# Last normalisation of each branch on ScalarE, o^T split beside the last heads, one more step ahead of the compressed transposes

## Chip, core and metric

The kernel runs on one core of a Trainium2 chip. The metric is the device time of one execution in microseconds (us). The engines are TensorE (PE in the profile; its weight loads are PEld), VectorE (DVE), ScalarE (ACT), GpSimd (POOL) and SyncE (SP, which issues most DMAs). Each engine takes its instructions in the order in which the program has put them into its queue.

## What is computed

A decoder trunk of two layers on x (512 tokens, width 1024). Each layer is a token mixer of two parallel branches, RetNet retention and NSA sparse attention, and then a SwiGLU FFN. The change touches the NSA branch alone. Cut to that branch, the reference is:

```python
lc = einsum('bghqd,bgnd->bghqn', qx, kc) * scale + head_bias(dc)      # compressed keys, 31 per group
pc = masked_softmax(lc, dc >= 0);  oc = einsum('bghqn,bgnd->bghqd', pc, vc)
ps = masked_softmax(ls, ds >= 0);  os_ = einsum('bghqm,bgqmd->bghqd', ps, vsel)   # selected blocks
pw = masked_softmax(lw, in_window); ow = einsum('bghql,bgld->bghqd', pw, vw)      # sliding window
out = gx[..., 0:1] * oc + gx[..., 1:2] * os_ + gx[..., 2:3] * ow
y_nsa = o_n @ w_o_nsa[i]
```

With 512 tokens, 8 blocks of 64 and a top-8 choice, every block is selected, and the window of 512 covers every earlier token. So the selected and the window branch are causal softmaxes over all tokens, each with its own keys and values.

## The kernel before

Every float32 product is made of three matmuls of a high and a low half (`mm3`, lines 122 to 124: weight high by activation high, low by high, high by low). The halves come from `split` (lines 79 and 80): ScalarE rounds a copy to the high half, VectorE subtracts to get the low half. `cut` does that to the weights that a DMA brought, into tiles `wh` and `wl`, of which three pairs exist.

`nsa` runs 16 heads in a software pipeline, one iteration a head. In an iteration stand the scores of head n (`nsa_scores`), the transposes and value products of head n-1 (`nsa_values`), the end of head n-2 (`nsa_finish`), and, to keep TensorE busy, pieces of other projections (`gate_steps`, the tiles f). `merge` interleaves these generators: a generator that is said to have so many steps gets its steps at even distances in its span of the iteration. The framework's scheduler then fixes each engine's queue.

- `nsa_scores`: for each of two branches and four blocks of 128 query rows, the scores go to a PSUM bank a (two exist), VectorE adds the bias and finds the maximum (line 509), ScalarE makes the exponential and its sum (line 510). The four blocks are 128, 256, 384 and 512 keys wide. After the last, VectorE turns the sums into factors sm (lines 533 to 536) and multiplies all eight blocks by them (line 540).
- `nsa_values`: TensorE transposes the normalised p into a bank t (line 560), ScalarE and VectorE split it into two tiles pt, and TensorE multiplies them with the values into a bank o (lines 552 and 553, high and low half).
- `nsa_cmp`, once for four heads (a quad): the compressed branch. Its scores are transposed, biased on VectorE (line 458), the maximum is found (line 462, VectorE) and subtracted (line 463, GpSimd), the exponential made (line 465, ScalarE), masked (line 466, GpSimd), summed (line 469, VectorE), and multiplied by the gate over the sum (line 476, GpSimd). Then TensorE transposes the result cz (line 480), and it is split into pc. The plan gives it 10 steps.
- `nsa_finish`: one more product with pc into bank o (line 574), then the two halves of the bank are added into the tile ot (lines 578 and 579). Two heads share one ot, so eight of them hold o^T.

After the loop, the eight ot are split into oh and ol (called from `nsa`, executed at lines 79 and 80), and the projection with w_o_nsa begins, eight times 24 matmuls.

Of the kernel before, what the change touches and what calls it, by code (L numbers as in the profile page):

```python
# [22 lines left out]
HN = 16  # L23
# [8 lines left out]
class Builder:  # L32
# [403 lines left out]
    def nsa_cmp(self, quad, qs, heads, pc):  # L436
        nc = self.nc
        ps = self.mm()
        for s, (qh, ql) in enumerate(qs):
            kz = self.kcz[s % 2][:, 96 - 32 * s : 224 - 32 * s]  # L440
            nc.tensor.matmul(ps, kz, qh, start=s == 0, stop=False)
            nc.tensor.matmul(ps, kz, ql, start=False, stop=s == 3)
        yield
        st = self.u("cst")
        nc.scalar.activation(st, ps, AF.Copy)
        pt = self.tp()
        for i in range(NT):
            nc.tensor.transpose(pt[:, i * P : (i + 1) * P], st[:, i * P : (i + 1) * P], self.ident)
        yield
        z = self.u("cz")  # L450
        z4 = z.rearrange("p (i s n) -> p i s n", i=NT, s=4)
        p4 = pt.rearrange("p (i s n) -> p i s n", i=NT, s=4)
        nc.gpsimd.memset(z, NEG)
        for i in range(NT):
            n = min(NCMP, 7 + 8 * i)
            for s in range(4):
                bias = self.backwards(heads[4 * quad + s]["strip"], 96 + P * i, n, 16)
                nc.vector.tensor_tensor(z4[:, i, s, :n], p4[:, i, s, :n], bias, ALU.add)
            yield
        z3 = z.rearrange("p (c n) -> p c n", n=32)  # L460
        mx = self.small("cmx", 16)
        nc.vector.tensor_reduce(mx, z3, AX.X, ALU.max)
        nc.gpsimd.tensor_tensor(z3, z3, mx[:, :, None].broadcast_to([P, 16, 32]), ALU.subtract)
        yield
        nc.scalar.activation(z, z, AF.Exp)
        nc.gpsimd.tensor_tensor(z4, z4, self.cmask[:, :, None, :].broadcast_to([P, NT, 4, 32]), ALU.mult)
        yield
        sm = self.small("csm", 16)
        nc.vector.tensor_reduce(sm, z3, AX.X, ALU.add)
        nc.vector.tensor_scalar(sm, sm, 1e-30, None, ALU.max)  # L470
        nc.vector.reciprocal(sm, sm)
        s4 = sm.rearrange("p (i a b) -> p i a b", a=2, b=2)
        for b in range(2):
            h0 = 2 * quad + 8 * b
            nc.vector.tensor_tensor(s4[:, :, :, b], s4[:, :, :, b], self.gate[:, :, h0 : h0 + 2, 0], ALU.mult)
        nc.gpsimd.tensor_tensor(z3, z3, sm[:, :, None].broadcast_to([P, 16, 32]), ALU.mult)
        yield
        pt2 = self.tp()
        for i in range(NT):
            nc.tensor.transpose(pt2[:, i * P : (i + 1) * P], z[:, i * P : (i + 1) * P], self.ident)  # L480
        yield

        for r, o in ((slice(0, 64), slice(64, P)), (slice(64, P), slice(0, 64))):
            x = self.u("pc", F32R)
            self.split(x[r], x[o], pt2[r])
            pc.append(x)


    def nsa_scores(self, st):
        nc = self.nc  # L490
        g = st["h"] // 8
        qh, ql = st["q"]
        ks = self.ks[g]
        strip = st["strip"]
        pr = st["p"] = [[None] * NT for _ in range(2)]
        nmx = self.small("nmx", 2 * NT)
        sm = self.small("sm", 2 * NT)


        p1 = self.tile("p", NPB)  # L500
        for br in range(2):
            p2, p3 = self.tile("p", NPB), self.tile("p", NPB)
            pr[br] = [p2[:, 3 * P :], p1[:, br * 2 * P : (br + 1) * 2 * P], p2[:, : 3 * P], p3]

        def soft(br, i, src):
            w = (i + 1) * P
            p = pr[br][i]
            c = slice(br * NT + i, br * NT + i + 1)
            nc.vector.tensor_tensor_reduce(p, src, self.backwards(strip, w - 1, w), -1.0, BIG, ALU.add, ALU.min, nmx[:, c])  # L509
            nc.scalar.activation(p, p, AF.Exp, scale=-1.0, bias=nmx[:, c], accum_out=sm[:, c])  # L510

        for i in range(2):
            w = (i + 1) * P
            ts = slice(i * P, w)
            ps = self.bank("a")
            dst = ps[:, : 2 * w].rearrange("p (b n) -> p b n", b=2)
            nc.tensor.matmul(dst, qh[:, ts], ks[:, :, :w], start=True, stop=False)
            nc.tensor.matmul(dst, ql[:, ts], ks[:, :, :w], start=False, stop=True)
            for br in range(2):
                soft(br, i, ps[:, br * w : (br + 1) * w])  # L520
            yield

        for br in range(2):
            for i in range(2, NT):
                w = (i + 1) * P
                ts = slice(i * P, w)
                ps = self.bank("a")
                nc.tensor.matmul(ps[:, :w], qh[:, ts], ks[:, br, :w], start=True, stop=False)  # L528
                nc.tensor.matmul(ps[:, :w], ql[:, ts], ks[:, br, :w], start=False, stop=True)  # L529
                soft(br, i, ps[:, :w])  # L530
                yield

        nc.vector.tensor_scalar(sm, sm, 1e-30, None, ALU.max)
        nc.vector.reciprocal(sm, sm)
        sv = sm.rearrange("p (b t) -> p b t", b=2)
        nc.vector.tensor_tensor(sv, sv, self.gate[:, :, st["h"], 1:].rearrange("p t b -> p b t"), ALU.mult)
        for br in range(2):
            for i in range(NT):
                c = br * NT + i
                nc.vector.tensor_scalar(pr[br][i], pr[br][i], sm[:, c : c + 1], None, ALU.mult)  # L540


    def nsa_values(self, st):
# [27 lines left out]
    def nsa_finish(self, st):  # L571
        nc = self.nc
        po, b, s = st["po"], st["h"] // 8, st["s"]
        nc.tensor.matmul(po, self.vc[:, b, s % 2], st["pc"][s // 2], start=False, stop=True)
        if b == 0:
            self.ot = self.u("ot")
        dst = self.ot[64 * b : 64 * b + 64]
        nc.scalar.activation(dst, po[64:128], AF.Copy)
        nc.vector.tensor_tensor(dst, po[0:64], dst, ALU.add)
        yield  # L580
        if b == 1:
            self.os.append(self.ot)

    def gate_steps(self, l, h):

# [42 lines left out]
    def nsa(self, l, h):  # L628
# [2 lines left out]
        q0 = self.nsa_q(l, h, 0, qs[0])  # L631
        self.ks, self.vs, self.gate = self.nsa_kv(l, h, q0)
        self.cycle = NCYCLE
        self.os = []
        heads = []
        fill = self.gate_steps(l, h)

        pcs = [[] for _ in range(4)]

        prep, plan = {}, [(1, 1, lambda: self.nsa_cmp(0, qs[0], heads, pcs[0]), 10)]  # L640
        for quad in range(1, 4):
            n = 4 * quad
            plan.append((n - QAT[0], QAT[1], lambda quad=quad: self.nsa_q(l, h, quad, qs[quad]), 18))
            plan.append((n, 1, lambda quad=quad: self.nsa_cmp(quad, qs[quad], heads, pcs[quad]), 10))
        for n0, span, make, steps in plan:
            g = make()
            for i in range(span):
# [5 lines left out]
        for n in range(HN + 2):  # L653
            gens = []
            if n == 0 or n % 4 == 3 and n + 1 < HN:
                for m in range(4):
                    st = heads[(n + 3) // 4 * 4 + m]
                    st["strip"] = self.bias_strip(st["h"])
            if n < HN:
                heads[n]["q"] = qs[n // 4][n % 4]  # L660
                gens.append((self.nsa_scores(heads[n]), 6, *AT["scores"]))
            if 0 < n <= HN:
                gens.append((self.nsa_values(heads[n - 1]), 8 + LAG, *AT["values"]))
            if n > 1:
                gens.append((self.nsa_finish(heads[n - 2]), 1, *AT["finish"]))
            gens.append((self.take(fill, FILL[n]), FILL[n], *AT["fill"]))
            gens += prep.get(n, [])
            self.merge(gens)
        for _ in fill:
            pass  # L670
        self.cycle = CYCLE
        w = self.a["w_o_nsa"][l]
        os = []
        for ot in self.os:
            os.append((self.u("oh", F32R), self.u("ol", F32R)))
            self.split(*os[-1], ot)
        for c in range(4):
            wv = self.chunk([(lambda v, g=g: v[g * 64 : g * 64 + 64], w[g * 512 : g * 512 + 512, c * 256 : c * 256 + 256]
                              .rearrange("(t d) n -> d t n", d=64)) for g in range(2)], KD, 256)
            for j in range(2):  # L680
                ps = self.proj_t(wv, j, os)
                yt = self.u("yn")
                nc.vector.scalar_tensor_tensor(yt, self.ld("gb", self.gs[KD + 2 * c + j]), 1.0, ps, ALU.add, ALU.mult)
                nc.scalar.dma_start(self.ys[2 * c + j], yt)
# [353 lines left out]
```

## Time and profile before

| | us |
|---|---|
| median of 3 runs (2425.92 to 2429.57) | 2428.91 |
| the profiled execution, its own time | 2427.7 |
| span of the profiled execution, first to last instruction | 2425.8 |
| TensorE busy in the span | 2371.8 (98%) |
| VectorE busy | 1410.7 (58%) |
| ScalarE busy | 1029.9 (42%) |
| GpSimd busy | 258.8 (11%) |

The profile gives each engine's busy time. Matmuls overlap in TensorE's pipeline, and their ends are modelled, so that two matmuls that start 0.23 us apart are each shown as 0.39 us. The distance of starts is the pace. The chain of work that ended last lies to 89% on TensorE, to 6% on VectorE and to 3% on ScalarE. The heads of the first layer run from about 85 to 416 us, those of the second from about 1285 to 1613 us; the projections of o^T follow right behind.

### The profile page before, as it was taken

The page shows a single profiled execution, that of the slowest core. Times are in us where ns is not written, and L with a number is a line of the kernel's source. Part 1 is how long each engine was busy: PE and PEld are TensorE (multiplying, and loading weights), DVE is VectorE, ACT ScalarE, POOL GpSimd, SP SyncE. Part 2 cuts the span into 40 slices and gives each one's busy share as a digit, 9 for nine tenths or more (in the row PEclk, how much of TensorE's full clock was granted, in tenths as well). Part 3 has the DMA queues.
Part 4 walks back from the last instruction along what each step waited for, and adds up shares of the span by engine and source line. Part 5 has one row for each costly group of instructions (what it writes and reads, how often), then busy time and mean ns, then how long its engine had stood idle before and what let it go on. Part 6 is the DMA issues. An engine that isn't in the chain of part 4 may idle for free.

```text
span 2425.8 us, 29172 instructions
## 1 busy us (share of the span) xinstructions
PE 2371.8 (98%) x11042; PEld 1938.4 (80%) x11042; DVE 1410.7 (58%) x2779; ACT 1029.9 (42%) x1862; POOL 258.8 (11%) x224
## 2 busy tenths in 40 slices
PE   7999999999999999999989999999999999999998
PEld 5877777888887888888878777778888878888887
DVE  6788887354574643333577888853555755434334
ACT  5676675233333422222356766742333333322222
POOL 2000000010020110110200000001100202101010
PEclk9999999999999999999999999999999999999999
DMA  7533124522342522322544322244233534223221
GB/s 209 149 89 84 57 74 100 166 90 91 109 148 88 166 89 91 101 94 94 147 142 125 96 68 65 79 110 146 92 102 98 164 114 135 87 87 104 87 96 61
DMA packets 234173, 260.37 MB, mean 107 GB/s; under 512 B 42213, under 2 KB 178437, under 8 KB 234032
## 3 DMA queue, kind: packets, MB, share of 16 engines
q1 hardware_dynamic: 220688, 236.93, 32.3%
q10 hardware_dynamic: 13152, 21.37, 2.4%
q8 instruction: 87, 1.43, 0.2%
q14 instruction: 54, 0.44, 0.1%
q0 software_dynamic: 192, 0.21, 0.0%
HBM read 235.36 MB, written 23.11 MB: 107 GB/s over the span
## 4 chain that ended last, share of the span: by engine, by line
PE 89%; DVE 6%; ACT 3%; issue 1%; POOL 1%; DMA 0%; SPq 0%; POOLq 0%; ACTq 0%; DVEq 0%
PE f L122 11%; PE f L123 11%; PE f L124 11%; PE o L123 8%; PE a L123 8%; PE o L122 8%; PE a L122 8%; PE o L124 8%; PE a L124 7%; PE t L560 2%; DVE p L540 1%; PE o L553 1%; PE o L552 1%; DVE wl L80 1%; PE a L528 1%
## 5 line engine op out<-in xcount | busy, mean ns | idle before, releaser
L79 ACT ACTIVATE wh<-wr 128x1024 fp32r<-128x1024 f32 (+3 forms) x406 | 397.9, 981 | 972.4 <-PE f L123 255.3
L80 DVE TENSOR_TENSOR wl<-wr,wh 128x1024 fp32r<-128x1024 f32 (+3 forms) x406 | 464.0, 1147 | 225.1 <-ACT wh L79 222.1
L122 PE MATMUL f<-hh,wh 128*128 128x512 f32 x936 | 373.9, 399 | 3.0 <-ACT wh L79 2.9
L123 PE MATMUL f<-hl,wh 128*128 128x512 f32 x936 | 371.0, 396 | 0.0
L124 PE MATMUL f<-hh,wl 128*128 128x512 f32 x936 | 369.3, 395 | 1.2 <-DVE wl L80 1.1
L124 PEld LDWEIGHTS f<-hh,wl 128*128 128x128 f32 x936 | 176.9, 189 | 41.5 <-DVE wl L80 3.6
L122 PEld LDWEIGHTS f<-hh,wh 128*128 128x128 f32 x936 | 177.0, 189 | 38.2 <-ACT wh L79 4.7
L123 PEld LDWEIGHTS f<-hl,wh 128*128 128x128 f32 x936 | 177.3, 189 | 30.5
L510 ACT ACTIVATE p<-p,nmx 128x512 f32<-128x512 f32 (+3 forms) x256 | 142.4, 557 | 67.1 <-DVE nmx L509 64.9
L80 DVE TENSOR_TENSOR pt<-t,pt 128x512 fp32r<-128x512 f32 (+3 forms) x256 | 123.2, 485 | 51.0 <-ACT pt L79 49.5
L79 ACT ACTIVATE pt<-t 128x512 fp32r<-128x512 f32 (+3 forms) x256 | 109.1, 429 | 76.0 <-PE t L560 73.0
L862 POOL TENSOR_TENSOR fa<-fa,rb 128x512 f32<-128x512 f32 x44 | 77.5, 1762 | 562.3 <-ACT fa L861 562.3
L123 PE MATMUL a<-hl,wh 128*128 128x512 f32 x336 | 132.5, 394 | 0.0
L122 PE MATMUL a<-hh,wh 128*128 128x512 f32 x336 | 132.2, 394 | 0.0
L509 DVE CUSTOM_DVE_ANT_0 p<-a,strip 128x512 f32<-128x512 f32 (+3 forms) x256 | 120.2, 484 | 19.4 <-PE a L529 12.0
L124 PE MATMUL a<-hh,wl 128*128 128x512 f32 x336 | 131.2, 390 | 0.0
L123 PE MATMUL o<-hl,wh 128*128 128x512 f32 x328 | 129.3, 394 | 0.0
L122 PE MATMUL o<-hh,wh 128*128 128x512 f32 x328 | 128.9, 393 | 0.0
L124 PE MATMUL o<-hh,wl 128*128 128x512 f32 x328 | 128.0, 390 | 0.0
L560 PE MATMUL t<-ident,p 128*128 128x128 f32 x640 | 113.5, 273 | 0.2
L560 PEld LDWEIGHTS t<-ident,p 128*128 128x128 f32 x640 | 80.5, 140 | 25.3 <-issue 3.1
L552 PE MATMUL o<-pt,vs 128*128 128x512 f32 (+3 forms) x256 | 91.5, 361 | 1.5 <-ACT pt L79 1.5
(404 smaller groups left out, 4832.4 us busy)
## 6 DMA issues: line engine op xcount, KB each, us to landing
wr<-in_w_in SPq DMA_DIRECT2D x66, 1024.0 KB, 5.3
wr<-in_w_ffn_in SPq DMA_DIRECT2D x44, 1024.0 KB, 5.1
wr<-in_w_ffn_out SPq DMA_DIRECT2D x18, 1024.0 KB, 5.0
wr<-in_w_o_ret SPq DMA_DIRECT2D x16, 1024.0 KB, 5.1
wr<-in_w_in SPq DMA_DIRECT2D x36, 256.0 KB, 4.6
strip<-bv SPq DMA_DIRECT2D x32, 256.0 KB, 4.4
gs<-mt ACTq DMA_DIRECT2D x32, 256.0 KB, 2.0
wr<-in_w_o_nsa SPq DMA_DIRECT2D x16, 512.0 KB, 6.5
```

Of the source, the lines that this page charges most:

```text
L79: self.nc.scalar.activation(hi, src, AF.Copy)
L80: (eng or self.nc.vector).tensor_sub(lo, src, hi.bitcast(F32))
L122: self.nc.tensor.matmul(ps, lh, rh, start=start and i == 0, stop=False)
L123: self.nc.tensor.matmul(ps, lh, rl, start=False, stop=False)
L124: self.nc.tensor.matmul(ps, ll, rh, start=False, stop=stop and i == n - 1)
L509: nc.vector.tensor_tensor_reduce(p, src, self.backwards(strip, w - 1, w), -1.0, BIG, ALU.add, ALU.min, nmx[:, c])
L510: nc.scalar.activation(p, p, AF.Exp, scale=-1.0, bias=nmx[:, c], accum_out=sm[:, c])
L528: nc.tensor.matmul(ps[:, :w], qh[:, ts], ks[:, br, :w], start=True, stop=False)
L540: nc.vector.tensor_scalar(pr[br][i], pr[br][i], sm[:, c : c + 1], None, ALU.mult)
L552: nc.tensor.matmul(po[:, j * P :], lhs, th, start=br == 0 and j == 0, stop=False)
L560: nc.tensor.transpose(pt[:, (i - j) * P : (i - j + 1) * P], pr[br][i][:, j * P : (j + 1) * P], self.ident)
L862: nc.gpsimd.tensor_mul(t, t, self.rb)
```

## The change

1. In `nsa_scores` the widest block of each branch (512 keys, two a head) is multiplied by its factor on ScalarE (an activation Copy with a column as scale) and not on VectorE.
2. A new generator `nsa_os` splits parts of o^T. It runs as one more generator in the last two iterations (up to part 3 in the first of them, up to part 6 in the second); the other two parts are split behind the loop.
3. `nsa_cmp` yields twice ahead of its transposes, and the plan gives it 11 steps.

```diff
         nc.gpsimd.tensor_tensor(z3, z3, sm[:, :, None].broadcast_to([P, 16, 32]), ALU.mult)
         yield
+        yield
         pt2 = self.tp()
...
-                nc.vector.tensor_scalar(pr[br][i], pr[br][i], sm[:, c : c + 1], None, ALU.mult)
+                if i == NT - 1:
+                    nc.scalar.activation(pr[br][i], pr[br][i], AF.Copy, scale=sm[:, c : c + 1])
+                else:
+                    nc.vector.tensor_scalar(pr[br][i], pr[br][i], sm[:, c : c + 1], None, ALU.mult)
...
+    def nsa_os(self, upto):
+
+        for n in range(len(self.oss), upto):
+            self.oss.append((self.u("oh", F32R), self.u("ol", F32R)))
+            self.split(*self.oss[n], self.os[n])
+            yield
...
-        prep, plan = {}, [(1, 1, lambda: self.nsa_cmp(0, qs[0], heads, pcs[0]), 10)]
+        prep, plan = {}, [(1, 1, lambda: self.nsa_cmp(0, qs[0], heads, pcs[0]), 11)]
...
-            plan.append((n, 1, lambda quad=quad: self.nsa_cmp(quad, qs[quad], heads, pcs[quad]), 10))
+            plan.append((n, 1, lambda quad=quad: self.nsa_cmp(quad, qs[quad], heads, pcs[quad]), 11))
...
+            if n >= HN:
+                upto = 3 * (n - HN + 1)
+                gens.append((self.nsa_os(upto), upto, 0, 1))
             self.merge(gens)
...
-        os = []
-        for ot in self.os:
-            os.append((self.u("oh", F32R), self.u("ol", F32R)))
-            self.split(*os[-1], ot)
+        for _ in self.nsa_os(HN // 2):
+            pass
...
-                ps = self.proj_t(wv, j, os)
+                ps = self.proj_t(wv, j, self.oss)
```

The scheduler moves instructions with it. TensorE where the projection of o^T begins in the first layer (oh and ol are the halves of o^T; o, a and f behind L122 to L124 are the banks that are written), before:

```order
L124 MATMUL f_4390<-hh_153,wl_4340 128x512
L122 MATMUL o_4467<-oh_4424,wh_4459 128x512
L122 MATMUL a_4497<-oh_4424,wh_4463 128x512
L122 MATMUL f_4538<-oh_4424,wh_4530 128x512
L123 MATMUL o_4467<-ol_4425,wh_4459 128x512
L124 MATMUL o_4467<-oh_4424,wl_4460 128x512
L122 MATMUL o_4467<-oh_4428,wh_4459 128x512
```

and now:

```order
L124 MATMUL f_4410<-hh_153,wl_4348 128x512
L122 MATMUL o_4467<-oh_4249,wh_4459 128x512
L123 MATMUL o_4467<-ol_4250,wh_4459 128x512
L124 MATMUL o_4467<-oh_4249,wl_4460 128x512
L122 MATMUL o_4467<-oh_4319,wh_4459 128x512
L123 MATMUL o_4467<-ol_4320,wh_4459 128x512
L124 MATMUL o_4467<-oh_4319,wl_4460 128x512
```

The first output is now made in one go, where three outputs were begun side by side before.

VectorE at the second quad of the first layer, from the normalisation to the sum of the compressed branch, before:

```order
L536 TENSOR_TENSOR sm_1653<-sm_1653,gate_624 128x8
L80 TENSOR_TENSOR wl_2070<-wr_2067,wh_2069 128x1024
L540 TENSOR_SCALAR p_1655<-p_1655,sm_1653 128x128
L540 TENSOR_SCALAR p_1654<-p_1654,sm_1653 128x256
L540 TENSOR_SCALAR p_1655<-p_1655,sm_1653 128x384
L540 TENSOR_SCALAR p_1656<-p_1656,sm_1653 128x512
L540 TENSOR_SCALAR p_1657<-p_1657,sm_1653 128x128
L540 TENSOR_SCALAR p_1654<-p_1654,sm_1653 128x256
L540 TENSOR_SCALAR p_1657<-p_1657,sm_1653 128x384
L540 TENSOR_SCALAR p_1658<-p_1658,sm_1653 128x512
L80 TENSOR_TENSOR pt_1852<-t_1849,pt_1851 128x128
L579 TENSOR_TENSOR ot_1858<-o_1426,ot_1858 64x512
```

and now:

```order
L80 TENSOR_TENSOR wl_2070<-wr_2067,wh_2069 128x1024
L80 TENSOR_TENSOR pt_1812<-t_1808,pt_1811 128x256
L534 TENSOR_SCALAR sm_1653<-sm_1653 128x8
L535 RECIPROCAL sm_1653<-sm_1653 128x8
L537 TENSOR_TENSOR sm_1653<-sm_1653,gate_624 128x8
L544 TENSOR_SCALAR p_1655<-p_1655,sm_1653 128x128
L544 TENSOR_SCALAR p_1654<-p_1654,sm_1653 128x256
L544 TENSOR_SCALAR p_1655<-p_1655,sm_1653 128x384
L544 TENSOR_SCALAR p_1657<-p_1657,sm_1653 128x128
L544 TENSOR_SCALAR p_1654<-p_1654,sm_1653 128x256
L544 TENSOR_SCALAR p_1657<-p_1657,sm_1653 128x384
L469 TENSOR_REDUCE csm_1876<-cz_1725 128x16
```

The two blocks of 512 have left the run, and the sum csm follows it at once; before it stood behind the split of pt and the sum ot.

TensorE at the same quad, up to the transposes of the compressed result cz, before:

```order
L122 MATMUL f_1838<-hh_153,wh_1830 128x512
L123 MATMUL f_1838<-hl_154,wh_1830 128x512
L528 MATMUL a_1951<-ks_251,qh_1412 128x384
L529 MATMUL a_1951<-ks_251,ql_1413 128x384
L124 MATMUL f_1838<-hh_153,wl_1831 128x512
L122 MATMUL f_1976<-hh_117,wh_1834 128x512
L123 MATMUL f_1976<-hl_118,wh_1834 128x512
L480 MATMUL t_1883<-ident,cz_1728 128x128 x4
```

and now:

```order
L124 MATMUL f_1842<-hh_149,wl_1835 128x512
L529 MATMUL a_1951<-ks_251,qh_1412 128x384
L530 MATMUL a_1951<-ks_251,ql_1413 128x384
L122 MATMUL f_1842<-hh_153,wh_1834 128x512
L481 MATMUL t_1883<-ident,cz_1725 128x128 x4
```

Four matmuls of 512 columns that stood ahead of the transposes stand behind them now. At the fourth quad the same happens; at the first and the third the transposes keep their place.

## Rows read from the trace of the kernel before

**Rows 1.** Three stretches: bounds, length, then busy time (instructions) of each engine
```profile
85.00:420.00 335.00, 325.36 (x1666) 263.43 (x1664) 271.26 (x770) 219.03 (x521) 15.71 (x15) 1.00 0.32 88
420.00:520.00 100.00, 100.00 (x436) 81.63 (x437) 46.59 (x67) 28.17 (x37) 9.33 (x9) 0.99 0.44 137
...
1285.00:1617.00 332.00, 322.36 (x1654) 261.29 (x1652) 268.35 (x761) 217.51 (x516) 15.70 (x15) 1.00 0.32 88
```

**Rows 2.** TensorE's waits, 85 to 420 us: for whom, total us, times, longest
```profile
PE o L553 <- DVE pt L80: 3.0, 3, 1.7
PE a L528 <- DVE nmx L509: 2.1, 2, 1.4
PE o L122 <- ACT oh L79: 2.0, 1, 2.0
...
PE t L480 <- POOL cz L476: 0.7, 3, 0.2
PE o L123 <- DVE ol L80: 0.4, 1, 0.4
```

**Rows 3.** TensorE's timeline around the projection's begin, both layers (start, us, instruction, [idle])
```profile
416.09 0.40 PE L124 MATMUL f<-hh,wl 128*128 128x512 f32 x1
418.45 0.50 PE L122 MATMUL o<-oh,wh 128*128 128x512 f32 x1 [1.96 <-ACT oh L79]
...
422.93 0.39 PE L124 MATMUL a<-oh,wl 128*128 128x512 f32 x1
...
1613.49 0.40 PE L124 MATMUL f<-hh,wl 128*128 128x512 f32 x1
...
1621.01 0.40 PE L123 MATMUL o<-ol,wh 128*128 128x512 f32 x1
```

**Rows 4.** Stretches there; after POOL's busy time stands the granted clock
```profile
416.00:419.00 3.00, 1.04 (x5) 0.54 (x4) 2.77 (x4) 2.63 (x4) 0.00 (x0) 1.00 1.10 287
419.00:423.00 4.00, 3.56 (x10) 2.53 (x9) 4.00 (x8) 3.23 (x6) 0.00 (x0) 0.57 0.47 111
```

**Rows 5.** ScalarE's and VectorE's timelines there
```profile
403.21 1.06 ACT L79 ACTIVATE wh<-wr 128x1024 fp32r<-128x1024 f32 x1 [0.84 <-PE f L123]
...
417.78 1.13 ACT L79 ACTIVATE oh<-ot 128x512 fp32r<-128x512 f32 x2
...
419.12 4.90 DVE L80 TENSOR_TENSOR ol<-ot,oh 128x512 fp32r<-128x512 f32 x8
```

**Rows 6.** Groups by form: the multiplication removed, and ScalarE's nearest to the one added
```profile
L540 DVE TENSOR_SCALAR p<-p,sm 128x512 f32<-128x512 f32 x32 | 16.4, 514 | 0.0
...
L941 ACT ACTIVATE p<-p,fr 128x512 f32<-128x512 f32 x4 | 2.9, 724 | 3.6 <-POOL fr L934 3.6
```

**Rows 7.** Timeline at the first quad of the first layer
```profile
120.66 2.46 DVE L540 TENSOR_SCALAR p<-p,sm 128x128 f32<-128x128 f32 x8
...
122.13 0.22 PE L552 MATMUL o<-pt,vs 128*128 128x128 f32 x1
...
123.38 0.33 PE L553 MATMUL o<-pt,vs 128*128 128x128 f32 x1 [1.03 <-DVE pt L80]
```

**Rows 8.** Timeline at the second quad of the first layer
```profile
181.52 3.54 DVE L540 TENSOR_SCALAR p<-p,sm 128x128 f32<-128x128 f32 x8
...
181.73 1.28 POOL L466 TENSOR_TENSOR cz<-cz,cmask 128x512 f32<-128x512 f32 x1 [1.29 <-ACT cz L465]
...
185.32 0.33 PE L553 MATMUL o<-pt,vs 128*128 128x128 f32 x1 [1.72 <-DVE pt L80]
...
187.71 1.05 POOL L476 TENSOR_TENSOR cz<-cz,csm 128x512 f32<-128x512 f32 x1 [4.70 <-DVE csm L475]
...
188.82 0.66 PE L480 MATMUL t<-ident,cz 128*128 128x128 f32 x4 [0.23 <-POOL cz L476]
```

**Rows 9.** TensorE at the third and fourth quad of the first layer
```profile
264.98 0.41 PE L528 MATMUL a<-ks,qh 128*128 128x384 f32 x1 [1.41 <-DVE nmx L509]
...
343.48 0.41 PE L528 MATMUL a<-ks,qh 128*128 128x384 f32 x1 [0.67 <-DVE nmx L509]
...
345.20 0.66 PE L480 MATMUL t<-ident,cz 128*128 128x128 f32 x4 [0.22 <-POOL cz L476]
```

More of the change, by code (lines that the diff above doesn't have):

```diff
@@ L633, in nsa @@
         self.cycle = NCYCLE
-        self.os = []
+        self.os, self.oss = [], []
         heads = []
```

## The prediction

> **What bounds the kernel now.** I read the busy times by stretch first. TensorE is the bound nearly everywhere: where nothing holds it, 436 matmuls take 100 us, 0.229 us each [rows 1]. In the heads it is idle for 9.6 us of 335 in the first layer and for 9.6 of 332 in the second [rows 1], so the change, which takes no matmul away, can win only what TensorE loses there and at the begin of the projection that follows. VectorE is busy for 271 us of those 335 and ScalarE for 219 [rows 1]; neither is the bound over the stretch, but in short runs VectorE is late. The list of TensorE's waits names them: 3.0 us for the low half of pt, 2.1 us for a score bank that VectorE frees, 0.7 us for GpSimd's compressed result, 2.0 and 0.4 us for the halves of o^T [rows 2]. The second layer repeats the first, wait by wait, so each place counts twice.
>
> **The projection of o^T.** The last matmul of the fill starts at 416.09. The next one waits for ScalarE's first oh and starts at 418.45 [rows 3]. In 416 to 419 TensorE is busy for 1.04 us of 3, and in 419 to 423 the granted clock is 0.57, so much of that stretch ran at 1.2 GHz and not at 2.4 [rows 4]. At 422.93 the pace is back. Between 416.09 and 422.93 lie 11 starts, which at 0.229 would take 2.52 us; they took 6.84. The place costs 4.32 us. In the second layer it is 13 starts from 1613.49 to 1621.01, 7.52 less 2.98, or 4.54 us [rows 3]. Both: 8.9 us.
>
> What is late there after the change? The first weight tile of the projection is cut at 403.21 already [rows 5], and by the new order six of the eight parts are split earlier, in queues that are waiting for TensorE's fill. Only parts 7 and 8 are split behind the loop. They take the place of the first two of before: ScalarE has them at 417.78 plus 1.13, VectorE at 419.12 plus twice 0.61 (4.90 for eight), or 420.35 [rows 5]. TensorE, which now makes the first output in one go, needs part 7 after 18 matmuls, at 416.3 plus 4.1 or 420.4, its low half one matmul later, and part 8 at 421.1. So nothing is late by more than a few tenths, TensorE never idles, and I see no reason for the clock to fall. I take the whole 8.9 us. The bounds are 6, if each layer keeps a wait of over 1 us, and 8.9.
>
> **The normalisation.** Per head, VectorE loses two instructions of 0.51 us [rows 6]; in an undisturbed run of eight that takes 2.46 us [rows 7], an instruction adds between 0.31 (an eighth of it) and 0.51, and I take 0.40 for the widest, so the run becomes 1.66 us. ScalarE gains two. The added form, a Copy of 128x512 with a column as scale, stands in the trace at 0.72 us [rows 6]; 64 of them are 46 us on an engine with a third of the stretch free. They begin when VectorE's factors are ready, which is when VectorE's own run begins, and end 1.44 us later, ahead of VectorE's 1.66. So the next transposes come 0.8 us earlier. What queues behind them on ScalarE is above all the high half of the last pt of the head before, a block of 128, which TensorE's line 552 waits for; its low half stands behind VectorE's run anyway.
>
> The Trainium skill, page "ScalarE: Activation LUTs", section "Rules for kernel authors", speaks against this edit: multiplications belong on VectorE. The rows agree that the instruction gets dearer (0.72 against 0.51), by 13 us of engine time in all; by that rule the edit would lose, and my sum differs because neither engine is the bound.
>
> First quad: the run at 120.66 ends at 122.3, and the high half that TensorE wants at 122.13 is ready at 120.66 plus 1.44 plus 0.28, at 122.4. The low half follows at 122.7, where before it let line 553 start at 123.38 [rows 7]. Gain 0.7 us.
>
> Second quad: the run of eight takes 3.54 us and not 2.46, with GpSimd's mask of 1.28 us inside it, and TensorE waits 1.72 us for the low half behind it [rows 8]. But another wait comes next: the chain of the compressed branch, sum, factors, GpSimd's product at 187.71, ends 1.05 us later, and only then can TensorE transpose, at 188.82 [rows 8]. In the new order the run is 0.8 us shorter and the sum stands right behind it, but four matmuls (0.92 us) have been moved behind the transposes, so TensorE comes to them sooner and waits there instead. The chain gets earlier by 0.8 to 1.9 us, the higher end if GpSimd's mask no longer delays VectorE by 1.1. The net is -0.1 to +1.0; I take 0.5, the middle.
>
> The Trainium skill, page "SBUF — State Buffer", section "Who interferes with whom", says that VectorE and GpSimd share a port pair as an exclusive lock, so that one blocks for the other's whole instruction. The 3.54 beside 2.46 us agrees; six multiplications would still meet the mask, and by that rule alone the second quad would give the lower end, -0.1.
>
> Third quad: TensorE's wait of 1.41 us for the score bank [rows 9] goes with VectorE's shorter run, but in ScalarE's new order both multiplications (1.44 us) stand ahead of the compressed exponential, so the sum behind the mask is later. Between -0.6 and +0.8; I take 0.2. Fourth quad: only the two multiplications leave VectorE's order, so the chain and with it 345.20 get 0.8 us earlier, but here too four matmuls have moved behind the transposes: -0.1. The 0.67 us wait there [rows 9] goes, and one for GpSimd takes its place.
>
> The extra step itself is thus nearly nothing: with 11 steps the parts ahead of the transposes come earlier, but the transposes themselves don't come later on TensorE.
>
> The other heads have small waits, of which some of the third wait for pt (3.0 less 1.03 and 1.72 [rows 2, 7, 8]) should go: 0.3. Sum per layer: 0.7 + 0.5 + 0.2 - 0.1 + 0.3 = 1.6 us; both layers 3.2.
>
> **Sum.** 8.9 + 3.2 = 12.1 us. The profiled execution took 2427.7 us, span 2425.8; it would take 2415.6. The median of the runs, 2428.9, lies 1.2 higher; from it, 2416.8. I say 2417.
>
> **Rivals.** (a) The compressed chain eats all that the heads win: GpSimd's product stays where it is, TensorE only waits at the transposes and not before. For it speaks that in three of four quads the transposes already wait for GpSimd (0.7 us in all [rows 2]). Heads 0, or somewhat below: -8.9 to -7, about 2421. (b) All of the heads' waits for VectorE and GpSimd go, 3.0 + 2.1 + 0.7 = 5.8 us a layer [rows 2], 11.6 in both: -20.5, about 2408. Against it speaks the order of the quads. (c) Slower: ScalarE's two multiplications wait for the factors with the rest of ScalarE's queue behind them, and TensorE stands for the high half of the pt of 128 in every head. With 32 heads, this eats the 8.9 us when it costs 0.28 us a head; at 0.6 us it is 19 less 9, plus 10, about 2439. The first quad above shows 0.2 to 0.3 us at one head that has little slack, but there VectorE was later still before, and the wait list shows only three waits for pt's low half in 16 heads [rows 2], so most heads have slack. (d) The change doesn't do what it says at the projection: parts 7 and 8, or the sixth, come so late that TensorE still idles and the clock still falls. Then 2 to 4 us in all are left, about 2426.
>
> **How the numbers follow.** The forecast (2413 to 2419.5) has 0.60, (a) 0.20, (b) 0.08, (c) 0.05, (d) 0.07. The range 2410 to 2423 holds the forecast, (a) and what lies between the forecast and (b). A run of this kernel can be told from no change at about 0.2%, 4.9 us, so below 2424: the forecast, (a), (b) and a share of (d) make 0.90 for faster, the rest of (d) 0.06 for the same; 0.04 for slower.
>
> **What would show it.** Right: no TensorE wait for oh or ol, a granted clock of 1.00 behind the fill, and the first output's 24 matmuls 0.23 us apart; waits for pt's low half below 1 us in a quad; at the second and fourth quad a longer wait of the transposes for GpSimd than 0.23. Wrong: a wait of over 0.3 us at line 552's successor for ScalarE in many heads (c), or a clock below 1 after the last head (d). If the transposes of cz do not wait at all, the quads were priced too low.

## The result

The changed kernel takes 2411.47 us (median of four executions, 2410.8 to 2412.95), the kernel before 2428.19 beside it. The ratio is 0.9939, with a 95% interval of 0.9927 to 0.9951: faster, by 16.7 us. The profiled execution took 2411.87 us, its span is 2409.8, 16.0 less than before. On a second chip, beside other kernels, it took 2410.19 against 2426.14, ratio 0.9935 (0.9921 to 0.9948).

TensorE's waits in the heads and behind them, 85 to 425 us, in the changed kernel (line waited at, releaser, us in total, times, longest); they stand against [rows 2]:

```profile
PE o L556 <- ACT pt L79: 1.6, 4, 0.5
PE a L529 <- DVE nmx L510: 1.4, 2, 0.8
PE t L481 <- POOL cz L476: 1.0, 3, 0.6
```

The waits for the halves of o^T and for pt's low half are gone; waits for pt's high half, 0.7 us before, are 1.6 now.

Four stretches of the changed kernel, as in [rows 1, 4] (bounds, length, busy time and instructions of PE, PEld, DVE, ACT, POOL, granted clock, DMA share, GB/s):

```profile
85.00:420.00 335.00, 330.53 (x1696) 269.25 (x1695) 263.46 (x746) 243.27 (x560) 15.64 (x15) 1.00 0.32 89
414.00:416.00 2.00, 2.00 (x11) 1.63 (x10) 1.76 (x3) 1.72 (x3) 0.00 (x0) 1.00 1.08 330
416.00:419.00 3.00, 3.00 (x15) 2.47 (x14) 2.41 (x4) 0.91 (x2) 0.00 (x0) 1.00 0.90 200
419.00:423.00 4.00, 4.00 (x19) 3.27 (x18) 1.91 (x2) 1.06 (x1) 0.00 (x0) 1.00 0.31 52
```

Behind the last head TensorE is busy all the time, at a granted clock of 1.00; before, [rows 4], it was busy for 1.04 of 3 us and then had 0.57. TensorE's timeline there (start, us, instruction), against [rows 3], and then ScalarE's and VectorE's splits of parts 7 and 8, against [rows 5]:

```profile
414.08 0.39 PE L124 MATMUL f<-hh,wl 128*128 128x512 f32 x1
414.31 0.39 PE L122 MATMUL o<-oh,wh 128*128 128x512 f32 x1
414.54 0.39 PE L123 MATMUL o<-ol,wh 128*128 128x512 f32 x1
414.77 0.39 PE L124 MATMUL o<-oh,wl 128*128 128x512 f32 x1
```

```profile
415.77 1.14 ACT L79 ACTIVATE oh<-ot 128x512 fp32r<-128x512 f32 x2
...
417.12 1.29 DVE L80 TENSOR_TENSOR ol<-ot,oh 128x512 fp32r<-128x512 f32 x2
```

The starts are 0.23 us apart from the last fill on, and the two late parts are ready at 417.8 and 418.4, where TensorE needs the seventh at 414.31 plus 4.1, or 418.4.

**Where the 16 us lie.** The heads of the two layers repeat to 0.1 us, so the program can be cut into stretches by the starts of single instructions: the heads, from the first `f<-qh,kcz` (101.19 us before) to the last head's `o<-pc,cv` (414.72), and what follows up to the second output of the projection (VectorE's second `yn`, 432.06). In the changed kernel these are 102.51, 412.71 and 425.50. The table gives the change of each stretch against the kernel before, in us; "rest" is all that lies outside (the first 101 us, the FFNs, the ends). Its rows are explained below.

| kernel | heads, layer 1 | layer 2 | behind them, 1 | 2 | rest | median us (before beside it) |
|---|---|---|---|---|---|---|
| changed | -3.33 | -3.35 | -4.55 | -4.93 | +0.1 | 2411.47 (2428.19) |
| the same on another chip | -3.41 | -3.35 | -4.55 | -4.93 | +1.8 | 2410.19 (2426.14) |
| os_only | -0.09 | -0.11 | -4.55 | -4.93 | -1.3 | 2418.10 (2425.96) |
| act_only | -2.92 | -2.92 | -0.11 | -0.51 | 0.0 | 2420.65 (2425.96) |
| step_only | -1.23 | -1.13 | +0.24 | -0.74 | -1.0 | 2422.55 (2425.96) |
| no_step | -2.86 | -2.82 | -4.55 | -4.94 | -1.6 | 2411.67 (2425.96) |
| os_three | -0.07 | -0.10 | -4.32 | -4.69 | -0.8 | 2420.08 (2426.90) |
| one_br | -3.03 | -2.97 | -4.55 | -4.93 | -1.1 | 2410.97 (2426.90) |
| wide_384 | +1.55 | +1.59 | -4.55 | -4.93 | -0.8 | 2422.87 (2426.90) |
| prod_dve | -3.98 | -3.95 | -4.55 | -4.93 | +2.3 | 2409.95 (2426.90) |
| one_prod | -3.61 | -3.62 | -4.55 | -4.93 | -1.7 | 2410.02 (2426.14) |
| mask_prod | -6.65 | -6.73 | -4.55 | -4.93 | -2.6 | 2404.39 (2426.14) |
| one_mask_prod | -7.02 | -6.98 | -4.55 | -4.93 | -2.3 | 2404.03 (2426.14) |

So the heads gave 6.7 us, where 3.2 were forecast, and the begin of the projection 9.5, where 8.9 were. The rest moves by -2.6 to +2.3 us between executions, in code that no edit touches. The stretches come from one profiled execution of each kernel. The medians moved by 0.6 us more to 2.4 us less than the four stretches together: os_only's, for instance, by 7.9 us where its stretches have 9.7.

### The profile page after: what moved, and what is told of

Same layout as the page of the kernel before. It is cut to its first block, busy times and chain, and to the rows that moved or that the text cites. A ratio compares the mean times of both kernels' runs of the same rounds, so it can differ in the third digit from the quotient of the medians.

```text
span 2409.8 us, 29134 instructions
## 1 busy us (share of the span) xinstructions
PE 2364.8 (98%) x11042; PEld 1936.3 (80%) x11042; DVE 1386.1 (58%) x2715; ACT 1070.7 (44%) x1926; POOL 258.2 (11%) x224
## 4 chain that ended last, share of the span: by engine, by line
PE 90%; ACT 4%; DVE 4%; issue 1%; POOL 1%; DMA 0%; SPq 0%; ACTq 0%; POOLq 0%
PE f L122 12%; PE f L123 12%; PE f L124 12%; PE a L123 8%; PE a L122 8%; PE o L122 8%; PE o L123 8%; PE o L124 8%; PE a L124 8%; PE t L564 2%; PE o L556 1%; PE o L557 1%; ACT wh L79 1%; PE a L529 1%; PE a L530 1%
## 5 line engine op out<-in xcount | busy, mean ns | idle before, releaser
L122 PE MATMUL f<-hh,wh 128*128 128x512 f32 x936 | 373.1, 399 | 3.2 <-ACT wh L79 3.2
L124 PE MATMUL f<-hh,wl 128*128 128x512 f32 x936 | 368.1, 394 | 1.2 <-DVE wl L80 1.1
L124 PEld LDWEIGHTS f<-hh,wl 128*128 128x128 f32 x936 | 176.4, 188 | 41.9 <-DVE wl L80 3.6
L122 PEld LDWEIGHTS f<-hh,wh 128*128 128x128 f32 x936 | 176.4, 188 | 37.7 <-ACT wh L79 5.0
L122 PE MATMUL a<-hh,wh 128*128 128x512 f32 x336 | 132.4, 394 | 0.0
L124 PE MATMUL a<-hh,wl 128*128 128x512 f32 x336 | 131.2, 390 | 0.0
L122 PE MATMUL o<-hh,wh 128*128 128x512 f32 x328 | 129.0, 393 | 0.0
L124 PE MATMUL o<-hh,wl 128*128 128x512 f32 x328 | 127.9, 390 | 0.0
```

What stands on the lines that cost most here:

```text
L122: self.nc.tensor.matmul(ps, lh, rh, start=start and i == 0, stop=False)
L124: self.nc.tensor.matmul(ps, ll, rh, start=False, stop=stop and i == n - 1)
```

## The experiments

**One part at a time.** os_only is the kernel before with `nsa_os` alone:

```diff
+            if n >= HN:
+                upto = 3 * (n - HN + 1)
+                gens.append((self.nsa_os(upto), upto, 0, 1))
```

> The kernel before with part 2 of the change alone: the halves of o^T made beside the last two heads. Theory (the parts add): TensorE's wait of 2.0 us for oh and the clock of 0.57 behind it go in both layers, 4.3 + 4.5 = 8.9 us, and the heads up to the last two stay as before: span 2425.8 - 8.9 = 2417 us, within 1 us. Rival (the parts need each other: the splits find room on VectorE and ScalarE only because the heads are lighter there): a wait for oh or ol, or a later end of the last heads, stays, and the gain is 5 us or less, span 2421 or more.

Measured: heads as before, 4.55 and 4.93 us behind them, the same as in the changed kernel; ratio 0.9968 (0.9956 to 0.9979). The parts don't need each other here, and the theory stands; its span, 2414.9, is 1.1 below the 2416 to 2418 that were expected, mostly since the rest came out 1.3 shorter. Of each figure 0.23 us is one matmul of the third output, which stood in this stretch before and stands later now; without it they are 4.3 and 4.7.

act_only is the kernel before with the multiplication alone:

```diff
-                nc.vector.tensor_scalar(pr[br][i], pr[br][i], sm[:, c : c + 1], None, ALU.mult)
+                if i == NT - 1:
+                    nc.scalar.activation(pr[br][i], pr[br][i], AF.Copy, scale=sm[:, c : c + 1])
+                else:
+                    nc.vector.tensor_scalar(pr[br][i], pr[br][i], sm[:, c : c + 1], None, ALU.mult)
```

> The kernel before with part 1 alone: the widest block of each branch multiplied by its factor on ScalarE. Theory (the multiplication is what the heads win): the heads get 3.4 us shorter in each layer, as in the changed kernel, span 2425.8 - 6.8 = 2419 us, within 1 us; the stretch behind the last head costs what it cost before. Rival (the extra step wins half of it, since the compressed chain decides at the transposes of cz): 3 to 4 us in both layers, span 2422 to 2423, and the transposes of cz wait longer for GpSimd than 0.23 us in the second and fourth quad.

Measured: 2.92 us a layer, 5.8 in both, less than the theory's 6.8 and far more than the rival's 3 to 4; ratio 0.9979 (0.9969 to 0.9988). One sign of the rival is there: the transposes of cz wait 0.59 and 0.56 us in the second and third quad. Behind the heads the wait of 1.96 us for oh is back, and with it the clock, 0.59 in the stretch from 415.90 to 420:

```profile
411.00:415.90 4.90, 2.99 (x14) 2.10 (x12) 2.40 (x3) 2.70 (x5) 0.00 (x0) 1.00 0.82 230
415.90:420.00 4.10, 3.74 (x9) 2.66 (x10) 4.10 (x8) 3.41 (x7) 0.00 (x0) 0.59 0.44 109
```

step_only is the kernel before with the second yield and eleven steps, no_step the changed kernel without them:

```diff
         nc.gpsimd.tensor_tensor(z3, z3, sm[:, :, None].broadcast_to([P, 16, 32]), ALU.mult)
         yield
+        yield
```

> The kernel before with part 3 alone: one more step ahead of the transposes of cz, eleven in the plan. Theory: nothing, span 2425.8 within 0.7 us, since VectorE's run of eight still holds up the sum. Rival (the step is what brings the compressed chain forward): 2 us or more of gain, half of the 6.8 us that the heads win, or, if TensorE now reaches other work that also waits for VectorE, up to 2 us slower.

> The changed kernel without part 3 (ten steps, one yield). Theory: as the changed kernel, span 2409.8 within 0.7 us. Rival (the step wins half of the heads' gain): 3 us slower, span about 2413.

Measured: the step alone gives 1.23 and 1.13 us (ratio 0.9985, 0.9976 to 0.9994). "Nothing" was wrong. Without it the changed kernel's heads are 0.5 us a layer longer, and its time is the same, since the rest came out 1.7 us shorter in that execution. The parts thus overlap: 2.9 and 1.2 alone, 3.35 together. What the step does is seen at two places. At the first quad VectorE's sum csm stands for GpSimd's mask, with the rest of VectorE's queue and at last the run of eight behind it. The kernel before, then step_only (VectorE):

```profile
115.80 0.69 DVE L469 TENSOR_REDUCE csm<-cz 128x16 f32<-128x512 f32 x1 [1.58 <-POOL cz L466]
```

```profile
115.49 0.69 DVE L469 TENSOR_REDUCE csm<-cz 128x16 f32<-128x512 f32 x1 [1.30 <-POOL cz L466]
```

Counted from the begin of the heads (101.19 and 101.25) the sum starts at 14.61 and at 14.24 us: with eleven steps the compressed chain is 0.37 us earlier there, and the run and TensorE behind it win as much (0.37 us at this quad). At the second quad, in step_only, GpSimd's mask begins before the run of eight and not inside it:

```profile
180.35 1.29 POOL L466 TENSOR_TENSOR cz<-cz,cmask 128x512 f32<-128x512 f32 x1 [1.45 <-ACT cz L465]
...
180.66 1.00 DVE L537 TENSOR_TENSOR sm<-sm,gate 128x8 f32<-128x8 f32 x1
181.70 2.46 DVE L541 TENSOR_SCALAR p<-p,sm 128x128 f32<-128x128 f32 x8
...
184.41 0.33 PE L554 MATMUL o<-pt,vs 128*128 128x128 f32 x1 [0.90 <-DVE pt L80]
```

The run takes 2.46 us where [rows 8] has 3.54, and TensorE's wait behind it falls from 1.72 to 0.90. Now the small multiplication ahead of the run, 128x8, takes 1.00 us and ends with the mask; in the first quad, where no GpSimd instruction is near, it takes 0.16. In the kernel before it was held up too, by GpSimd's subtraction ahead of the mask:

```profile
179.39 1.05 POOL L463 TENSOR_TENSOR cz<-cz,cmx 128x512 f32<-128x512 f32 x1 [31.73 <-DVE sm L534]
179.68 0.78 DVE L536 TENSOR_TENSOR sm<-sm,gate 128x8 f32<-128x8 f32 x1
```

So GpSimd cost VectorE 0.62 and 1.08 us before, 1.70 in all, and costs it 0.84 with the step: 0.86 less, about what TensorE's wait lost (0.82).

**How much of the widths.** one_br leaves one of the two blocks on VectorE, wide_384 moves the blocks of 384 keys as well:

```diff
-                if i == NT - 1:
+                if br == 1 and i == NT - 1:
```

```diff
-                if i == NT - 1:
+                if i >= NT - 2:
```

> The changed kernel with the widest block of the second branch alone on ScalarE, that of the first back on VectorE. Theory (the heads win what VectorE's run gets shorter, 0.4 us for each block, wherever it is late): half of what part 1 adds to part 3, between the heads with part 3 alone (1.2 us a layer) and the changed kernel (3.35): about 2.3 us a layer, span 2 us above the changed kernel, 2412. Rival (ScalarE's two multiplications hold up the high halves of pt, 1.6 us of waits a layer against 0.7 before, and one alone does not): the halved cost makes up for the halved gain, span 2410 or below.

> The changed kernel with the blocks of 384 keys on ScalarE as well: VectorE's run has four instructions and takes about 1.0 us, ScalarE's four take about 2.4. Theory (ScalarE's queue behind the multiplications is now the later one): TensorE's waits for the high half of pt grow from 1.6 us a layer to 3 or more, and the kernel is 1 to 4 us slower than the changed one, span 2411 to 2414. Rival (VectorE is still the late engine in the quads): 1 to 2 us faster, span 2408.

Measured: one block gives 3.0 us a layer, nearly as much as two; the forecast of half fell, and the rival's direction is right, though 3.0 is not more than 3.35. The rival's reason isn't borne out: TensorE's waits for pt's high half are still 1.4 us a layer in one_br (95 to 412 us), against 1.6. Four blocks give a loss of 1.6 us a layer, 4.9 against the changed kernel, 9.8 in both: the theory's sign, but far beyond its 1 to 4 us. Its place is another, too. TensorE's waits in the first layer's heads (95 to 412 us) of wide_384:

```profile
PE t L481 <- POOL cz L476: 3.6, 3, 2.1
PE o L556 <- ACT pt L79: 2.7, 6, 0.7
PE f L122 <- ACT wh L79: 0.7, 1, 0.7
```

The waits for pt's high half did grow to 2.7, but those for GpSimd's cz grew more, from 1.0 to 3.6. At the third quad, whose head is 0.9 us longer than in the changed kernel (all engines by time):

```profile
259.45 2.34 ACT L542 ACTIVATE p<-p,sm 128x384 f32<-128x384 f32 x4
...
261.70 0.62 ACT L465 ACTIVATE cz<-cz 128x512 f32<-128x512 f32 x1
...
262.39 1.31 POOL L466 TENSOR_TENSOR cz<-cz,cmask 128x512 f32<-128x512 f32 x1 [3.05 <-ACT cz L465]
...
265.41 1.22 DVE L80 TENSOR_TENSOR wl<-wr,wh 128x1024 fp32r<-128x1024 f32 x1
...
265.63 1.90 POOL L476 TENSOR_TENSOR cz<-cz,csm 128x512 f32<-128x512 f32 x1 [1.94 <-DVE csm L475]
...
267.59 0.66 PE L481 MATMUL t<-ident,cz 128*128 128x128 f32 x4 [2.09 <-POOL cz L476]
```

Here ScalarE's compressed exponential stands behind four multiplications, so mask, sum and product are late one after another. In the product GpSimd meets a VectorE instruction of two operands that began 0.22 us earlier (`wl`, 1.22 us), and takes 1.90 us where it mostly takes 1.05. This is near rival (c) of the prediction, a queue behind ScalarE's multiplications, at a dose that the change doesn't reach, though what is late here is the compressed exponential and not the pt of 128 that (c) names: with none, one, two and four blocks on ScalarE (the first is step_only) the heads change by -1.2, -3.0, -3.35 and +1.6 us a layer.

**How many parts of o^T.** os_three splits three parts beside the last head and five behind the loop:

```diff
-            if n >= HN:
-                upto = 3 * (n - HN + 1)
+            if n > HN:
+                upto = 3
```

> The kernel before with part 2 alone, but only three of the eight parts of o^T split beside the last head, five behind the loop. Theory (the wait and the low clock are one loss: TensorE idles, and the clock falls behind it): the fourth part's halves come about 1 us after TensorE has used the first three, so of the 4.3 to 4.5 us a layer some 1 to 2 are left, with a stretch below 1.00 only if TensorE idles: span 2417 to 2420, where all six parts gave 2415. Rival (the loss is set by how many parts stand behind the loop, whatever TensorE does): five eighths of it are left, 5.5 us in both layers. Third way (three parts cover the time in which the others are split): no wait, clock 1.00, span 2415 as with six.

Measured: 4.32 and 4.69 us, 0.23 less than with six parts, ratio 0.9973 (0.9962 to 0.9984). The third way holds: no wait, and the clock stays at 1.00. TensorE and VectorE there, with the two stretches:

```profile
418.01 0.40 PE L124 MATMUL o<-oh,wl 128*128 128x512 f32 x1
418.31 0.50 PE L122 MATMUL o<-oh,wh 128*128 128x512 f32 x1
418.65 0.39 PE L122 MATMUL a<-oh,wh 128*128 128x512 f32 x1
...
418.99 3.09 DVE L80 TENSOR_TENSOR ol<-ot,oh 128x512 fp32r<-128x512 f32 x5
```

```profile
416.00:418.00 2.00, 2.00 (x10) 1.65 (x9) 1.76 (x3) 1.85 (x3) 0.00 (x0) 1.00 1.10 329
418.00:422.00 4.00, 4.00 (x18) 2.93 (x17) 4.00 (x7) 2.46 (x5) 0.00 (x0) 1.00 0.49 118
```

The fourth part's low half is indeed late, behind 418.99. But the queue has the second output's matmuls (bank a) with the first three parts between, so TensorE goes on. My expectation of a 1 us wait used the changed kernel's order, in which the first output is made in one go; with three parts early the scheduler gives another.

**The compressed chain.** prod_dve moves the chain's last product to VectorE; mask_prod moves the mask too; one_prod and one_mask_prod are the same two with one of the widest blocks back on VectorE, as in one_br:

```diff
-        nc.gpsimd.tensor_tensor(z4, z4, self.cmask[:, :, None, :].broadcast_to([P, NT, 4, 32]), ALU.mult)
+        nc.vector.tensor_tensor(z4, z4, self.cmask[:, :, None, :].broadcast_to([P, NT, 4, 32]), ALU.mult)
...
-        nc.gpsimd.tensor_tensor(z3, z3, sm[:, :, None].broadcast_to([P, 16, 32]), ALU.mult)
+        nc.vector.tensor_tensor(z3, z3, sm[:, :, None].broadcast_to([P, 16, 32]), ALU.mult)
```

> The changed kernel with the last product of the compressed branch (the result by the gate over the sum) on VectorE, where it takes about 0.67 us, and not on GpSimd, where it takes 1.05. Theory (at the quads the compressed chain sets the end, as the waits for cz of 1.0 us a layer say): the transposes start 0.4 to 0.5 us earlier in each quad that waits, 1 us a layer at most, span 2408 to 2409. Rival (VectorE is the late engine): 0.6 us more on its queue holds up the next maxima, and TensorE's waits for score banks grow by as much: span as the changed kernel or 1 us above.

> The changed kernel once more, beside the three that follow, so that they stand on one chip. Theory: the heads from the first product of the first quad to the last head 3.3 us shorter in each layer than before, the stretch behind them 4.5 and 4.9; the span by what the first 100 us do, 2409 to 2411. Rival (part of the 16.7 us lies in the start-up, which differs from run to run): the same two terms, but the total between 15 and 18 us.

> The changed kernel with one of the two widest blocks back on VectorE and the last product of the compressed branch on VectorE. Theory (each of the two leaves the other's place alone: the one moves 0.3 us of loss, the other wins 0.6 us a layer): heads 3.6 us a layer shorter than before. Rival (VectorE, with 0.4 us more from the block and 0.7 from the product in the same run, is late again in the quads): 3.0 us a layer or less, waits for nmx above 1.5 us a layer.

> The changed kernel with both the mask (1.3 us on GpSimd, 1.8 in the fourth quad) and the last product of the compressed branch on VectorE, some 0.7 us each. Theory (GpSimd's instruction holds up VectorE's as well: the factors' multiplication of 128x8 took 1.02 us beside the mask and 0.16 in the first quad, where none runs): VectorE wins back about 0.85 us in the second to fourth quad and pays 0.7 for the mask, the chain gets 0.6 us shorter, heads 4.5 us a layer shorter than before, 0.5 beyond the product alone. Rival (the mask waits for ScalarE's exponential with VectorE's whole queue behind it): in the first to third quad VectorE stands up to 1 us, waits for nmx and pt grow, heads 3.5 us a layer or less.

> As the one before, with one of the two widest blocks back on VectorE. Theory: within 0.4 us a layer of it. Rival (VectorE is now the later engine by the mask, the product and the block): over 1 us a layer longer, waits for nmx and for the low half of pt.

Measured: the product alone wins 0.6 us a layer in the heads, within the 1 us that its theory allowed; the profiled execution's total doesn't show it, since the rest was 2.3 us longer there. The waits for cz are gone (0.07 us at the third quad, none else), but the transposes don't start earlier: at the second quad they begin 7.09 us behind the head's begin, against 7.01 in the changed kernel. Instead two more matmuls stand ahead of them in TensorE's queue at each of the last three quads (29, 33 and 32 against 27, 31 and 30). The rival fell: the waits for score banks stay at 1.4 us. one_prod has 3.6, as its theory said. The mask wins another 2.7 us a layer, five times what was expected of it: mask_prod takes 2404.39 us, ratio 0.9908 (0.9895 to 0.9922), against 0.9935 (0.9921 to 0.9948) of the changed kernel on the same chip, and beats both kernels by its stretches and by its time. one_mask_prod has 0.3 us a layer more, and 2404.03 us: the same within the intervals. TensorE's waits in the heads of mask_prod (95 to 412 us):

```profile
PE o L556 <- ACT pt L79: 1.1, 3, 0.4
PE f L442 <- ACT ql L431: 0.2, 1, 0.2
```

Those for score banks (nmx, 1.4 us) and for cz (1.0) are gone, 2.4 of the 3.3 us by which its heads are shorter than the changed kernel's. At the second quad, first in the changed kernel (VectorE, GpSimd, ScalarE and TensorE by time), then in mask_prod:

```profile
180.90 1.29 POOL L466 TENSOR_TENSOR cz<-cz,cmask 128x512 f32<-128x512 f32 x1 [1.45 <-ACT cz L465]
...
181.21 1.02 DVE L537 TENSOR_TENSOR sm<-sm,gate 128x8 f32<-128x8 f32 x1
...
182.26 1.34 ACT L542 ACTIVATE p<-p,sm 128x512 f32<-128x512 f32 x2 [1.44 <-DVE sm L537]
182.26 1.67 DVE L544 TENSOR_SCALAR p<-p,sm 128x128 f32<-128x128 f32 x6
...
183.81 0.33 PE L556 MATMUL o<-pt,vs 128*128 128x128 f32 x1 [0.54 <-ACT pt L79]
183.84 0.68 DVE L469 TENSOR_REDUCE csm<-cz 128x16 f32<-128x512 f32 x1
...
187.33 0.66 PE L481 MATMUL t<-ident,cz 128*128 128x128 f32 x4 [0.20 <-POOL cz L476]
```

```profile
178.57 0.69 DVE L466 TENSOR_TENSOR cz<-cz,cmask 128x512 f32<-128x512 f32 x1
...
179.29 0.69 DVE L469 TENSOR_REDUCE csm<-cz 128x16 f32<-128x512 f32 x1
...
179.90 0.16 DVE L537 TENSOR_TENSOR sm<-sm,gate 128x8 f32<-128x8 f32 x1
...
184.35 0.60 PE L481 MATMUL t<-ident,cz 128*128 128x128 f32 x4
```

The mask takes 0.69 us on VectorE, and the small multiplication 0.16 instead of 1.02: VectorE pays less than it had lost. The sum follows the mask at once. Against prod_dve the gain lies at the second, third and fourth quad, 1.0, 0.5 and 1.3 us. At the second and the fourth the small multiplication is 0.86 and 0.82 us shorter. At the third it is not (0.66 us, since GpSimd's subtraction, which stays, runs beside it); there VectorE's sum stood 0.59 us for GpSimd's mask in prod_dve and stands for nothing now, a price that the theory lacked. Why the 0.7 us of the mask on VectorE doesn't show in the gains was not taken apart further.

## Why the prediction was right, and where it was not

**The projection of o^T: right.** The step "I take the whole 8.9 us" holds. os_only alone gives it; in act_only and step_only, without the early splits, the wait for oh is back and the stretch moves by +0.24 to -0.74 us. In the changed kernel no wait for oh or ol is left, the first output's matmuls are 0.23 us apart, and the clock is 1.00. By starts it is 4.3 and 4.7 us, 9.0 against 8.9. That wait and clock are one loss is borne out from both sides: kernels with the wait (act_only) have the low clock, kernels without it (os_only, os_three) don't, in the same place and with the same matmuls but one.

**The heads: the mechanism right, the sum mis-sized**, 3.2 against 6.7 us in both layers. By place, in the first layer (against the kernel before, read at the heads' `o<-pc,cv`):

| | forecast | measured | act_only |
|---|---|---|---|
| first quad | 0.7 | 1.13 | 0.76 |
| second quad | 0.5 | 0.93, less 0.54 in the next two heads | 1.19, less 0.87 |
| third quad | 0.2 | 0.83 | 0.81 |
| fourth quad | -0.1 | 0.38 | 0.37 |
| other heads | 0.3 | 0.6 | 0.7 |

- "the run becomes 1.66 us", "end 1.44 us later": VectorE's six take 1.67, ScalarE's two 1.34. The prices were right. The Trainium skill, page "ScalarE: Activation LUTs", section "Rules for kernel authors", would have multiplications on VectorE; two blocks against that rule won 5.8 us, four lost.
- "The extra step itself is thus nearly nothing" failed. It is worth 1.2 us a layer alone and 0.5 beside the multiplication. The sentence saw that the earlier steps come sooner and priced that at nothing; but VectorE stands for GpSimd's mask in the first quad, and there the chain, VectorE's run and TensorE are all 0.37 us earlier. It is the whole difference to the forecast at that quad: 0.76 without it, 1.13 with it. In the second quad the step alone wins 0.9 more, as it puts the mask ahead of VectorE's run. Beside the multiplication little of that is left (0.1), since without the step the mask already comes behind the run there: in act_only the run takes 1.66 us, up to 182.82, and the mask starts at 182.85.
- Second quad: "the chain gets earlier by 0.8 to 1.9 us" held (GpSimd's product at 187.71 before, 186.22 now: 1.5, and 1.7 against the head's start, which is 0.2 later). What the sum lacked is the price behind: two waits for pt's high half of 0.5 and 0.3 us, at this head and a later one. This is rival (c) in small: such waits are 1.6 us a layer, 0.7 before.
- The Trainium skill, page "SBUF — State Buffer", section "Who interferes with whom", was read as the lower end, -0.1. The section says that a VectorE instruction with two SBUF inputs and a GpSimd instruction that reads SBUF exclude each other, and that whoever issues first makes the other wait. The traces agree, 1.02 us for 128x8 beside the mask and 0.16 without, and 1.90 against 1.05 with the roles exchanged. But which VectorE instruction meets the mask had changed, and the conclusion for the quad with it.
- Third quad: between the bounds of -0.6 and +0.8 I took 0.2, and it came out at the upper end. ScalarE's exponential did come later, and the mask with it, 1.05 us by the trace's time and 1.3 against the head's start. But the sum had not waited for the mask before; it stood behind VectorE's run, which ran into the mask (3.51 us, now 1.67), and it is 0.98 us earlier, 0.76 against the head's start. The bound that delayed the mask had slack.
- Fourth quad: "-0.1" took the four matmuls that moved behind the transposes as lost. Up to the transposes that is what happened: TensorE is there 0.79 us earlier, with 0.92 us less done. Behind them the kernel before has two places where TensorE starts 0.26 and 0.28 us later than the pace (after 350.63 and 353.55); in the changed kernel these are gone, and the moved matmuls stand in that stretch. Work moved behind a wait is lost only if TensorE has no other gaps there.
- The sign "a longer wait of the transposes for GpSimd than 0.23" in the second and fourth quad didn't show: 0.20 and 0.21, and 0.55 in the third.

**The rivals.** (a), the compressed chain eats the heads' gain, is refuted by the stretches. (b), all of the heads' waits go, did not happen: of 6.8 us a layer in the heads 4.0 are left. mask_prod comes near it, with 1.3. (c) is there in small at two blocks; at four ScalarE's queue decides, through cz (3.6 us) more than through pt's high half (2.7). (d) did not happen.

The time, 2411.47, lies in the range (2410 to 2423), near its low end, 5.5 us below the forecast and 1.5 below the band of 2413 to 2419.5 that had a chance of 0.60; faster was right.

## To carry to other kernels

Where TensorE stands at a hand-over between stages, a part of the next stage's preparation put into the earlier stage's idle places is worth the wait and the low clock behind it; three parts of eight were enough here, since the scheduler fills with other outputs. Of a short run on a late engine, move as much as makes another engine late next and no more: with the step's 1.2 us a layer in each figure, one block of eight gave 3.0, two 3.35, and four turned it into a loss of 1.6. Before giving GpSimd an elementwise product of two tiles to relieve VectorE, look at what VectorE does beside it: here it was slower there (1.3 against 0.7 us) and held up VectorE as well.

## What was not expected of the hardware

- A VectorE multiplication of 128x8 took 1.02 us beside GpSimd's mask and 0.16 alone; GpSimd's own product took 1.90 us beside a VectorE subtraction and 1.05 else. In these two the cost falls on the one that comes second, and it is not small for a small instruction.
- Outside the heads and the projection's begin, in code that no edit touches, profiled executions differ by up to 5 us (rest -2.6 to +2.3; +0.1 and +1.8 for the changed kernel itself), while the heads repeat to 0.1 us between layers, executions and chips. A change of 1 us is read from a stretch between two instructions, not from one total.
